# A hybrid decoder step: DeltaNet's keys, queries and values and the other heads' decayed keys turned by VectorE and DMA instead of TensorE

## Chip, core and metric

The kernel runs on one core of one Trainium2 chip. The time is the device time of one execution in microseconds (us); lower is better. A core has TensorE (PE: matmuls; PEld: its weight loads), VectorE (DVE), ScalarE (ACT), GpSimd (POOL) and SyncE (SP), which here issues every DMA. Each engine works off a queue of its own in order.

## What is computed

One layer of a decoder whose 16 heads are of three kinds, on 16 meta tokens + 1024 prompt tokens and on 8 samples of 8 tokens. Everything is float32; D is 2048 and a head has 128 channels.

```python
h = rmsnorm(x) ; proj = h @ w_in                      # 2048 x 8984
# 6 mLSTM heads (A): q, k, v, o and two gates; chunked, state C (128x128), n, m
P = exp(Dm - mt) * (q @ k.T);  num = a * (q @ C) + P @ v;  C_new = a_s * C + (w * k).T @ v
# 6 gated DeltaNet heads (B): a convolution of width 4 and silu over q, k, v, then q, k L2-normed
M = I + strict_tril(beta * decay * (k @ k.T));  solve M [U, Wk] = [beta v, beta e^G k]
W = U - Wk @ S;  o = e^G q @ S + Aqk @ W;  S_new = e^Ge S + (k e^(Ge-G)).T @ W
# 4 HGRN2 heads (C): per-channel forget gates
S_new = e^be S + (k e^(be-b)).T @ v
y = headRMSNorm(concat(heads)) * out_norm_w * silu(z);  out = x + y @ w_out  -> final rmsnorm
```

## The kernel before

The tokens are cut into two halves: half 0 has 80 sample and meta tokens (a small group) and 512 prompt tokens, half 1 the other 512 prompt tokens. The 512 are worked as a main group of four chunks of 128 (`NC = 4`). Activations lie with channels on partitions and tokens along the row; the recurrences also need some of them the other way round, a chunk's 128 tokens on partitions.

**Projection.** For each half, head by head in `ORDER` and tile by tile (k, q, v, o, z and so on; 128 columns of `w_in` each), `run_group` multiplies 16 slices of 128 rows. The weights come in pieces of four slices, 128x512: `w_raw` (and `o_raw` for `w_out`) loads a piece into a buffer `wraw` of the pool `wp` (four buffers), `feed_split` splits it into `whi` (ACT) and `wlo` (DVE, subtracting), and three products per slice go to `acc` (`oacc` for the output projection). `feed_ahead`, in the middle of each piece, lets the split run three pieces ahead and the load seven.

**Scans.** When a head's tiles are done, a generator (`mlstm_scan`, `gdn_scan`, `hgrn_scan`) does its recurrence. Its steps are woven between the weight matmuls by a planner (`Weave`, `Clock`) that adds up costs per engine while the program is written: a step runs when its due time, `ck.last + 0.4`, is reached on the planned TensorE clock; some steps set `ck.last` later. Scans run one after another in a queue; `finish` (the head's norm and gate) and `conv_post` (DeltaNet's convolution and silu) have queues of their own. `start_head` lets the head before the previous one run out (`weave.drain`). The framework then fixes the order of every engine's queue when the program is built.

**Row-wise tiles.** Two ways are in use. On TensorE: four transposes against `ident` into a PSUM bank, as for `pk` (mLSTM's k), `pck`, `pcq`, `pvb` (DeltaNet's k, q, v) and `pkh` (HGRN's decayed k). By VectorE and DMA, as for the values of mLSTM and HGRN, mLSTM's o and the scans' outputs: `V.transpose` turns 32x32 blocks, `turn_out` stores them to DRAM in four DMAs that put the blocks in place, and `turn_in` loads the turned tile in one.

**Buffers.** A tile's tag names its slot. Main-group tiles `gt("0")` to `gt("9")` have one slot each (`s0` to `s9`), shared by all scans; `kwall` and `Ball` share `sB`.

Of the kernel before, what the change touches and what calls it, by code (L numbers as in the profile page):

```python
# [14 lines left out]
P = 128  # L15
# [16 lines left out]
SQ = 32  # L32
# [159 lines left out]
def hybrid_step(ctx, tc, i, o):  # L192
# [25 lines left out]
    def bank(name):  # L218
        return ps.tile([P, 512], F32, tag="ps", name=name)
# [9 lines left out]


    def w_raw(col, g):
        raw = wp.tile([P, 512], F32, tag="wraw", name="wraw")
        v = raw.rearrange("p (k c) -> p k c", c=P)
        if col is None:
            V.memset(raw, 0.0)
            for src, at in ((C_AI, 0), (C_BB, 32), (C_AF, 64), (C_BA, 96)):
                DMA(v[:, :, at:at + HA], i["w_in"][0, 512 * g:512 * (g + 1), src:src + HA].rearrange("(k p) c -> p k c", p=P))
        else:
            DMA(v, i["w_in"][0, 512 * g:512 * (g + 1), col:col + P].rearrange("(k p) c -> p k c", p=P))
        return raw  # L240

    def o_raw(k, cg):
        raw = wp.tile([P, 512], F32, tag="wraw", name="wraw")
        DMA(raw, i["w_out"][0, P * k:P * (k + 1), 512 * cg:512 * (cg + 1)])
        return raw

# [182 lines left out]
    DMA(prows[0:72, :], i["gdn_conv_w"][0].rearrange("j (e c) -> (j e) c", c=P))  # L429
    DMA(prows[72:88, :], i["out_norm_w"][0].rearrange("(e c) -> e c", c=P))  # L430
    DMA(prows[88:92, :], i["hgrn_lower_bounds"][0].rearrange("(e c) -> e c", c=P))
    gsc = cp.tile([P, 1], F32, name="gsc")
    gbi = cp.tile([P, 1], F32, name="gbi")
    gn = cp.tile([P, 1], F32, name="gn")
    gli = cp.tile([P, 1], F32, name="gli")
    for t in (gsc, gbi, gn, gli):
        G.memset(t, 0.0)
    G.memset(gsc[RF], -1.0)
# [359 lines left out]
                S.activation(t[:, off:off + cnt], a, func, scale=scale)  # L798
        return t

    def turn_out(t, name):

        d = dp.tile([NC * NQ, SQ, NQ, SQ], F32, name=name)
        for q in range(NQ):
            DMA(d[:, :, q].rearrange("x j i -> j x i"), t[SQ * q:SQ * (q + 1), 0:HALF].rearrange("p (x i) -> p x i", i=SQ))
        return d
# [4 lines left out]
    def turned_evac(half, acc, tag, name, small):  # L811
        t = row(tag, name)
        for a, off, cnt in spans(half, acc):
            n = min(cnt, HALF - off)
            V.transpose(t[:, off:off + n], a[:, 0:n])
            if n < cnt:
                small(t[:, HALF:off + cnt], a[:, n:cnt])
        return t, turn_out(t, scratch_name(name))

    scratch_names = []  # L820

# [9 lines left out]
    def finish(half, head, outs, ssq, scale, zs):  # L831
        r = sp.tile([P, 16], F32, tag="hr", name="hr")
        for g in half.groups:
            V.tensor_scalar(r[0:g.n, g.idx], ssq[0:g.n, g.idx], scale / P, EPS, op0=ALU.mult, op1=ALU.add)
            G.tensor_tensor(r[0:g.n, 8 + g.at:8 + g.at + g.nt], r[0:g.n, g.idx], halfneg[0:g.n, 0:g.nt], op=ALU.pow)
        yield
        hrs = []
        for g, hx in zip(half.groups, outs):
            hr = gt("6", g)
            rb = r[0:g.n, 8 + g.at:8 + g.at + g.nt].unsqueeze(2).to_broadcast([g.n, g.nt, P])  # L840
            V.tensor_tensor(hr[0:g.n], hx[0:g.n], rb, op=ALU.mult)
            hrs.append(hr)
# [3 lines left out]
        d = turn_out(y, scratch_name("yd"))  # L846
# [118 lines left out]
    def mlstm_scan(half, h, kT, qT, vT, tho, zs, nm, em, st):  # L965
# [10 lines left out]
        Cn = state_A[h]  # L976
        Es, kws, v1s, ogs, hxs = [], [], [], [], []
        kwall = sp.tile([P, 5, P], F32, tag="sB", name="kwall", bufs=1)
        for g in half.groups:
            n = g.n  # L980
            pst = bank("pst")
            for c in range(g.nt):
                T.matmul(g.psum(pst, n)[:, c], g.col(kT, c), g.col(qT, c), start=True, stop=True)
            E = gt("0", g)
            for c in range(g.nt):
                S.activation(E[0:n, c, 0:n], g.col(nm, c)[0:n], AF.Exp, bias=cols[0:n, g.at + c, K_A, h:h + 1])
            ck.sync()
            V.tensor_tensor(E[0:n, :, 0:n], E[0:n, :, 0:n], g.psum(pst, n), op=ALU.mult)
            Es.append(E)
        yield  # L990
        for g in half.groups:
            n = g.n
            pk = bank("pk")
            for c in range(g.nt):
                T.transpose(g.psum(pk)[:, c], g.col(kT, c), ident)
            kw = kwall[:, g.idx]
            V.tensor_tensor(kw[0:n], g.psum(pk), gate_col(half, g, K_W, h), op=ALU.mult)
            kws.append(kw)
            v1 = gt("2", g, P + 1)
# [107 lines left out]
        G.tensor_copy(U[:, 0:3], hist[:, ei])  # L1107
        return U

    def conv_post(half, U, ei, Cv):  # L1110
        base = NB * (NS + 3)
        W = half.width
        co = sq("io", "co")
# [27 lines left out]
        yield  # L1141
        yield
        silu2(Cv[:, 0:W], U[:, 0:W], Cv[:, 0:W])

    def gdn_scan(half, h, ck_, cq, cv, zs, Gb, eG, bb, st):
        W = half.width
# [4 lines left out]
        qd = row("k", "qd")[:, 0:W]  # L1151
        nrm = sp.tile([P, 40], F32, tag="nrm", name="nrm", bufs=1)
        V.memset(nrm, 1.0)
        pks = []
        for g in gs:
            pk, pq = bank("pck"), bank("pcq")
            for c in range(g.nt):
                T.transpose(g.psum(pk)[:, c], g.col(ck_, c), ident)
            for c in range(g.nt):
                T.transpose(g.psum(pq)[:, c], g.col(cq, c), ident)  # L1160
            for off, src in ((0, pk), (5, pq)):
                for c in range(g.nt):
                    scr = sq("scr", "scrq", bufs=1)
                    S.activation(scr[0:g.n], g.psum(src)[:, c], AF.Square, accum_out=nrm[0:g.n, off + g.at + c:off + g.at + c + 1])
# [6 lines left out]
        yield  # L1171
        kns, Es = [], []
        for g, pk in zip(gs, pks):
            kn = gt("4", g)
            V.tensor_tensor(kn[0:g.n], g.psum(pk), nrm[0:g.n, 20 + g.at:20 + g.at + g.nt].unsqueeze(2).to_broadcast([g.n, g.nt, P]), op=ALU.mult)
            kns.append(kn)
        for g in gs:
            E = gt("0", g)
# [73 lines left out]
        def side():  # L1252
# [156 lines left out]
    def hgrn_scan(half, h, kT, lf, qT, vT, zs, st):  # L1409
# [97 lines left out]
        for g in gs:  # L1507
# [18 lines left out]
        Ss = gt("4", main)  # L1526
# [66 lines left out]
    def done_tile(half, name, what, acc):  # L1593
# [23 lines left out]
        elif kind == "B":  # L1617
# [5 lines left out]
            c["posts"].append(weave.add("post", conv_post(half, U, ei, t[what]), lag="V"))  # L1623
        else:
            if what == "f":
                cf = evac(half, acc, "f", "cf")[:, 0:half.width]
# [200 lines left out]
```

## Time and profile before

| | |
|---|---|
| median of 3 runs | 2525.41 us (2525.31 to 2526.97) |
| the profiled execution | 2525.14 us, its span 2523.4 us |
| PE busy | 2456.8 us (97%), 15702 matmuls |
| PEld / DVE / ACT / POOL busy | 2199.6 / 1427.0 / 1012.3 / 555.0 us |
| DMA engines | 53.9% for the queue that carries the data, 139 GB/s |
| half 0's projection and scans | to about 1185 us; half 1's to about 2118; then the output projection |

A line of a group reads: code line, engine, operation, tiles written <- read, shapes, count | busy time, mean ns of one | idle time of the engine before them and what ended it. All engine operations have one code line (L138), the helper that records them, so tiles tell them apart. Timeline rows give start, length, engine and operation, and in brackets how long the engine had been idle and what released it. "L239 <- DVE wlo" among SP's waits reads: the issue at line 239 waited for VectorE's instruction on wlo.

### The profile page before, as it was taken

What the parts mean: (1) busy time and instruction counts of PE and PEld (TensorE: products, weight loads), DVE (VectorE), ACT (ScalarE), POOL (GpSimd) and SP (SyncE); (2) the same over time, 40 slices, a digit from 0 to 9 for tenths busy, and PEclk for the clock granted to TensorE, in tenths of its full rate; (3) what the DMA queues carried; (4) which work ended last, traced back from release to release, by engine and by line L of the source; (5) the groups of instructions that cost most, each with busy time, mean ns of one, the idle gap of its engine ahead of it and who ended that gap; (6) DMA issues with size and microseconds to landing.
All of it is one profiled execution on the core that took longest, in us unless ns stands there. A gap on an engine that the chain in (4) does not pass through costs nothing.

```text
span 2523.4 us, 43205 instructions
## 1 busy us (share of the span) xinstructions
PE 2456.8 (97%) x15702; PEld 2199.6 (87%) x15702; DVE 1427.0 (57%) x2977; ACT 1012.3 (40%) x2476; POOL 555.0 (22%) x722
## 2 busy tenths in 40 slices
PE   6999999999999999999899999999999999999998
PEld 5899999999999999999687888888888888888886
DVE  7775656765746655556854556554554645323435
ACT  5643434343435333343643434333543334322324
POOL 5331211420314212213320103110320102211201
PEclk9999999999999999999999999999999999999999
DMA  5666655656545454448455445454554548636735
GB/s 129 157 143 147 154 135 122 166 135 133 144 97 143 97 128 115 118 105 225 115 134 122 119 121 130 120 132 100 131 128 111 130 118 264 175 83 195 259 96 184
DMA packets 681041, 350.77 MB, mean 139 GB/s; under 512 B 260004, under 2 KB 622076, under 8 KB 680828
## 3 DMA queue, kind: packets, MB, share of 16 engines
q1 hardware_dynamic: 680828, 348.01, 53.9%
q8 instruction: 123, 2.02, 0.3%
q14 instruction: 90, 0.74, 0.1%
HBM read 285.71 MB, written 62.19 MB: 138 GB/s over the span
## 4 chain that ended last, share of the span: by engine, by line
PE 74%; DMA 6%; issue 6%; DVE 5%; ACT 4%; POOL 3%; SPq 1%; POOLq 0%; DVEq 0%; ACTq 0%
PE acc L138 55%; PE oacc L138 8%; PE pa L138 1%; DVE wlo L138 1%; DMA wraw<-in_w_in_dram 1%; PE po L138 1%; POOL X L138 1%; PE pyy L138 1%; PE pz L138 1%; POOL res L138 1%; ACT whi L138 1%; PE pu L138 1%; ACT L138 1%; PE poh L138 1%; PE nd L138 1%
## 5 line engine op out<-in xcount | busy, mean ns | idle before, releaser
L138 DVE TENSOR_TENSOR wlo<-wraw,whi 128x512 fp32r<-128x512 f32 x720 | 528.4, 738 | 584.9 <-ACT whi L138 566.0
L138 PE MATMUL acc<-hA,whi 128*128 128x288 f32 (+1 forms) x4544 | 823.0, 303 | 11.5 <-ACT whi L138 7.0
L138 ACT CAST whi<-wraw 128x512 fp32r<-128x512 f32 x720 | 441.3, 618 | 879.8 <-PE acc L138 570.2
L138 PE MATMUL acc<-hB,whi 128*128 128x512 f32 x2272 | 723.8, 400 | 4.4 <-ACT whi L138 3.2
L138 PEld LDWEIGHTS acc<-hA,whi 128*128 128x128 f32 x4544 | 678.3, 191 | 17.5 <-ACT whi L138 8.4
L138 PE MATMUL acc<-hA,wlo 128*128 128x288 f32 x2240 | 488.9, 298 | 2.1 <-DVE wlo L138 2.0
L138 PEld LDWEIGHTS acc<-hB,whi 128*128 128x128 f32 x2272 | 411.2, 189 | 84.0 <-ACT whi L138 4.0
L138 PE MATMUL acc<-hB,wlo 128*128 128x512 f32 x1120 | 440.5, 393 | 5.1 <-DVE wlo L138 4.9
L138 PEld LDWEIGHTS acc<-hA,wlo 128*128 128x128 f32 x2240 | 367.1, 190 | 2.9 <-DVE wlo L138 2.9
L138 PE MATMUL oacc<-whi,y 128*128 128x512 f32 x1088 | 344.8, 391 | 1.7 <-ACT whi L138 1.6
L138 PEld LDWEIGHTS acc<-hB,wlo 128*128 128x128 f32 x1120 | 210.6, 188 | 55.9 <-DVE wlo L138 10.4
L138 PEld LDWEIGHTS oacc<-whi,y 128*128 128x128 f32 x1088 | 205.0, 188 | 45.6 <-ACT whi L138 3.4
L138 PE MATMUL oacc<-wlo,y 128*128 128x512 f32 x576 | 225.5, 392 | 2.1 <-DVE wlo L138 2.1
L138 PEld LDWEIGHTS oacc<-wlo,y 128*128 128x128 f32 x576 | 108.6, 189 | 26.1 <-DVE wlo L138 3.9
L138 POOL TENSOR_TENSOR res<-res,fnw 128x512 f32<-128x512 f32 (+1 forms) x34 | 54.3, 1624 | 255.3 <-ACT oscr L138 255.3
L138 POOL TENSOR_TENSOR qd<-qT,emb 128x512 f32<-128x512 f32 x12 | 16.8, 1403 | 355.9 <-PE po L138 355.9
L138 POOL TENSOR_TENSOR y<-y,zs 128x592 fp32r<-128x592 f32 (+1 forms) x32 | 45.5, 1420 | 92.4 <-ACT zs L138 62.8
L138 DVE TENSOR_TENSOR Yt<-Yc,Bb 128x60 f32<-128x60 f32 (+8 forms) x180 | 36.7, 204 | 39.4 <-DMA Bb<-db 34.4
L138 POOL TENSOR_TENSOR hr<-hr,halfneg 128x4 f32<-128x4 f32 (+1 forms) x48 | 47.4, 987 | 46.2 <-DVE hr L138 44.7
L138 POOL TENSOR_TENSOR X<-Ex,hk 128x256 f32<-128x256 f32 (+1 forms) x40 | 38.1, 953 | 87.8 <-PE pa L138 67.9
L138 POOL TENSOR_TENSOR nrm<-nrm,halfneg 128x10 f32<-128x10 f32 x12 | 23.5, 1955 | 122.6 <-DVE nrm L138 122.6
L138 DVE TENSOR_TENSOR Sx<-Sx,lf 128x256 f32<-128x256 f32 (+2 forms) x60 | 36.5, 613 | 20.2 <-ACT Ex L138 19.1
(410 smaller groups left out, 2805.8 us busy)
## 6 DMA issues: line engine op xcount, KB each, us to landing
wraw<-in_w_in_dram SPq DMA_DIRECT2D x564, 256.0 KB
wraw<-in_w_out_dram SPq DMA_DIRECT2D x144, 256.0 KB
y<-y SPq DMA_DIRECT2D x16, 576.0 KB
px<-in_x_prompt_dram SPq DMA_DIRECT2D x32, 256.0 KB
yd<-y SPq DMA_DIRECT2D x128, 64.0 KB
out_dram<-sst SPq DMA_DIRECT2D x16, 512.0 KB
s<-yd SPq DMA_DIRECT2D x32, 256.0 KB
y<-zs SPq DMA_DIRECT2D x32, 256.0 KB
```

Source lines behind the costliest of these rows:

```text
L138: return f(out, *a, **k)
```

## The change

Five tiles that were transposed on TensorE for the main group take the other way: DeltaNet's k, q, v, mLSTM's k, HGRN's decayed k. The small group of half 0 keeps TensorE. `turn` is new: a VectorE transpose into `uT` (one buffer) and `turn_out`. For DeltaNet it stands at the end of `conv_post`; the loads stand at the start of `gdn_scan`, with a yield and a due time 7 us later before the norms. In `mlstm_scan` the key's transpose stands ahead of the first matmuls, and the loads of k, v and o move into a step of their own after them, with a due time of 6 us. In `hgrn_scan` transpose and load are in one step, followed by 6 us. `wraw` gets a fifth buffer, and four single-column tiles become one tile of four columns.

```diff
     def w_raw(col, g):
-        raw = wp.tile([P, 512], F32, tag="wraw", name="wraw")
+        raw = wp.tile([P, 512], F32, tag="wraw", name="wraw", bufs=5)
...
-    gsc = cp.tile([P, 1], F32, name="gsc")
-    gbi = cp.tile([P, 1], F32, name="gbi")
-    gn = cp.tile([P, 1], F32, name="gn")
-    gli = cp.tile([P, 1], F32, name="gli")
+    gpar = cp.tile([P, 4], F32, name="gpar")
+    gsc, gbi, gn, gli = (gpar[:, n:n + 1] for n in range(4))
...
+    def turn(src, d):
+        t = sp.tile([P, HALF], F32, tag="uT", name="uT", bufs=1)
+        V.transpose(t, src)
+        turn_out(t, d)
+        return d
...
 # mlstm_scan
+        dk = turn(kT[:, 0:HALF], turn_tile("kd"))
         for g in half.groups:
...
             Es.append(E)
+        ck.last += 2.0
+        yield
+        v1m, og = gt("2", half.main, P + 1), gt("3", half.main)
+        turn_in(kwall[:, half.main.idx], dk)
+        turn_in(v1m[:, :, 0:P], vT[1])
+        turn_in(og, tho[1])
+        ck.last = ck.t["T"] + 6.0
         yield
         for g in half.groups:
             n = g.n
-            pk = bank("pk")
-            for c in range(g.nt):
-                T.transpose(g.psum(pk)[:, c], g.col(kT, c), ident)
-            kw = kwall[:, g.idx]
-            V.tensor_tensor(kw[0:n], g.psum(pk), gate_col(half, g, K_W, h), op=ALU.mult)
+            kw = pk = kwall[:, g.idx]
+            if g.small:
+                pk = bank("pk")[:, 0:P].unsqueeze(1)
+                T.transpose(pk[0:n, 0], g.col(kT, 0), ident)
+            V.tensor_tensor(kw[0:n], pk[0:n], gate_col(half, g, K_W, h), op=ALU.mult)
...
-            else:
-                turn_in(v1[:, :, 0:P], vT[1])
-                og = gt("3", g)
-                turn_in(og, tho[1])
 # conv_post, its last step
         silu2(Cv[:, 0:W], U[:, 0:W], Cv[:, 0:W])
+        turn(Cv[:, half.base:half.base + HALF], turned)
 # gdn_scan
+        (ck_, dk), (cq, dq), (cv, dv) = ck_, cq, cv
...
-            pk, pq = bank("pck"), bank("pcq")
-            for c in range(g.nt):
-                T.transpose(g.psum(pk)[:, c], g.col(ck_, c), ident)
-            for c in range(g.nt):
-                T.transpose(g.psum(pq)[:, c], g.col(cq, c), ident)
+            if g.small:
+                pk, pq = (bank(n)[0:g.n, 0:P].unsqueeze(1) for n in ("pck", "pcq"))
+                T.transpose(pk[:, 0], g.col(ck_, 0), ident)
+                T.transpose(pq[:, 0], g.col(cq, 0), ident)
+            else:
+                pk, pq, vm = gt("4", g), gt("9", g), gt("3", g)
+                turn_in(pk, dk)
+                turn_in(pq, dq)
+                turn_in(vm, dv)
+                ck.last = ck.t["T"] + 7.0
+                yield
...
-            kn = gt("4", g)
-            V.tensor_tensor(kn[0:g.n], g.psum(pk), nrm[...], op=ALU.mult)
+            kn = gt("4", g) if g.small else pk
+            V.tensor_tensor(kn[0:g.n], pk, nrm[...], op=ALU.mult)
...
-                pv = bank("pvb")
-                for c in range(g.nt):
-                    T.transpose(g.psum(pv)[:, c], g.col(cv, c), ident)
-                vb = gt("3", g)
-                V.tensor_tensor(vb[0:n], g.psum(pv), gate_col(half, g, K_HB, h), op=ALU.mult)
+                if g.small:
+                    pv = bank("pvb")[0:n, 0:P].unsqueeze(1)
+                    T.transpose(pv[:, 0], g.col(cv, 0), ident)
+                    vb = gt("3", g)
+                else:
+                    pv = vb = vm
+                V.tensor_tensor(vb[0:n], pv, gate_col(half, g, K_HB, h), op=ALU.mult)
 # hgrn_scan
+        dk = turn(kd[:, 0:HALF], turn_tile("kd"))
         for g in gs:
-            pt = bank("pkh")
-            for c in range(g.nt):
-                T.transpose(g.psum(pt)[:, c], g.col(kd, c), ident)
             kk = gt("3", g)
-            S.copy(kk[0:g.n], g.psum(pt))
+            if g.small:
+                pt = bank("pkh")
+                T.transpose(g.psum(pt)[:, 0], g.col(kd, 0), ident)
+                S.copy(kk[0:g.n], g.psum(pt))
+            else:
+                turn_in(kk, dk)
             kks.append(kk)
+        ck.last = ck.t["T"] + 6.0
         yield
```

More of the change, by code (lines that the diff above doesn't have):

```diff
@@ L242, in o_raw @@
     def o_raw(k, cg):
-        raw = wp.tile([P, 512], F32, tag="wraw", name="wraw")
+        raw = wp.tile([P, 512], F32, tag="wraw", name="wraw", bufs=5)
         DMA(raw, i["w_out"][0, P * k:P * (k + 1), 512 * cg:512 * (cg + 1)])
@@ L799, in evac, with turn_tile, turn_out @@
         return t
-    def turn_out(t, name):
-        d = dp.tile([NC * NQ, SQ, NQ, SQ], F32, name=name)
+    def turn_tile(name):
+        return dp.tile([NC * NQ, SQ, NQ, SQ], F32, name=scratch_name(name))
+    def turn(src, d):
[3 more added lines that the diff above has]
+        return d
+    def turn_out(t, d):
         for q in range(NQ):
@@ L817, in turned_evac @@
                 small(t[:, HALF:off + cnt], a[:, n:cnt])
-        return t, turn_out(t, scratch_name(name))
+        return t, turn_out(t, turn_tile(name))
     scratch_names = []
@@ L845, in finish @@
         V.transpose(y[:, 0:HALF], hrs[-1].rearrange("p c e -> p (c e)"))
-        d = turn_out(y, scratch_name("yd"))
+        d = turn_out(y, turn_tile("yd"))
         ck.last += 2.0
@@ L992, in mlstm_scan @@
             n = g.n
-            pk = bank("pk")
-            for c in range(g.nt):
-                T.transpose(g.psum(pk)[:, c], g.col(kT, c), ident)
-            kw = kwall[:, g.idx]
-            V.tensor_tensor(kw[0:n], g.psum(pk), gate_col(half, g, K_W, h), op=ALU.mult)
+            kw = pk = kwall[:, g.idx]
[3 more added lines that the diff above has]
+            V.tensor_tensor(kw[0:n], pk[0:n], gate_col(half, g, K_W, h), op=ALU.mult)
             kws.append(kw)
-            v1 = gt("2", g, P + 1)
+            v1 = gt("2", g, P + 1) if g.small else v1m
             G.memset(v1[0:n, :, P:P + 1], 1.0)
@@ L1108, in conv_evac, with conv_post @@
         return U
-    def conv_post(half, U, ei, Cv):
+    def conv_post(half, U, ei, Cv, turned):
         base = NB * (NS + 3)
@@ L1163, in gdn_scan @@
                     scr = sq("scr", "scrq", bufs=1)
-                    S.activation(scr[0:g.n], g.psum(src)[:, c], AF.Square, accum_out=nrm[0:g.n, off + g.at + c:off + g.at + c + 1])
+                    S.activation(scr[0:g.n], src[:, c], AF.Square, accum_out=nrm[0:g.n, off + g.at + c:off + g.at + c + 1])
             pks.append(pk)
@@ L1173, in gdn_scan @@
         for g, pk in zip(gs, pks):
[L1174 to L1175 removed]
+            kn = gt("4", g) if g.small else pk
+            V.tensor_tensor(kn[0:g.n], pk, nrm[0:g.n, 20 + g.at:20 + g.at + g.nt].unsqueeze(2).to_broadcast([g.n, g.nt, P]), op=ALU.mult)
             kns.append(kn)
@@ L1622, in done_tile @@
             t[what] = row({"k": "c", "q": "d", "v": "f"}[what], "C" + what)
-            c["posts"].append(weave.add("post", conv_post(half, U, ei, t[what]), lag="V"))
+            d = turn_tile("cd")
+            c["posts"].append(weave.add("post", conv_post(half, U, ei, t[what], d), lag="V"))
+            t[what] = t[what], d
         else:
```

## The prediction, made before the changed kernel had run

> **What bounds the kernel now.** I read the page first (busy shares), then the busy time by stretch, the waits of PE, the groups of the instructions that the change touches, and the timeline around them.
>
> ```profile
> PE 2456.8 (97%) x15702; PEld 2199.6 (87%) x15702; DVE 1427.0 (57%) x2977; ACT 1012.3 (40%) x2476; POOL 555.0 (22%) x722
> ```
>
> ```profile
> 650.00:700.00 50.00, 50.00 (x378) 49.81 (x377) 33.14 (x64) 20.36 (x61) 15.71 (x22) 1.00 0.57 148
> ...
> 1150.00:1200.00 50.00, 48.50 (x337) 43.73 (x335) 28.43 (x53) 14.85 (x34) 17.75 (x18) 1.00 0.88 247
> ...
> 2350.00:2400.00 50.00, 50.00 (x222) 41.40 (x221) 19.61 (x31) 14.45 (x28) 5.95 (x4) 1.00 0.83 279
> ```
>
> ```profile
> PE acc L138 <- ACT whi L138: 10.2, 8, 3.0
> PE acc L138 <- DVE wlo L138: 6.9, 8, 1.4
> ```
>
> The columns of the stretches are PE, PEld, DVE, ACT and POOL busy, PE's clock, the share of the DMA engines and GB/s. In stretches as far apart as 650 and 2350 us PE is busy for all 50 us, and its longest waits on the split weights come to 10.2 and 6.9 us in the whole run. So TensorE is the bound from end to end. An instruction taken off PE is worth its own time there, as long as nothing new makes PE wait. That is the whole question here.
>
> **What PE loses.** The change takes the full-chunk transposes off PE. Heads are counted by the code: DeltaNet's k, q and v, 6 heads x 2 halves x 4 chunks = 48 each; mLSTM's keys, 48; HGRN's decayed keys, 4 x 2 x 4 = 32. The groups show those counts:
>
> ```profile
> L138 PE MATMUL pcq<-ident,Cq 128*128 128x128 f32 x48 | 7.2, 273 | 0.0
> L138 PE MATMUL pk<-ident,kT 128*128 128x128 f32 x48 | 7.2, 272 | 0.0
> L138 PE MATMUL pvb<-ident,Cv 128*128 128x128 f32 x48 | 7.2, 272 | 0.0
> L138 PE MATMUL pck<-ident,Ck 128*128 128x128 f32 x48 | 7.2, 272 | 0.0
> ...
> L138 PE MATMUL pkh<-ident,hkd 128*128 128x128 f32 x32 | 4.8, 272 | 0.0
> ```
>
> That is 224 transposes; the small first group keeps its own. What does one cost? Three readings: 272 ns from start to end; 7.2/48 = 150 ns of busy time, with overlaps counted once; and what it really pushes back. The timeline gives the last:
>
> ```profile
> 336.31 0.47 PEld L138 LDWEIGHTS pck<-ident,Ck 128*128 128x128 f32 x4
> ...
> 336.75 0.47 PEld L138 LDWEIGHTS pcq<-ident,Cq 128*128 128x128 f32 x4
> ...
> 337.19 0.57 PEld L138 LDWEIGHTS acc<-hA,whi 128*128 128x128 f32 x4
> ...
> 1575.95 0.60 PE L138 MATMUL pkh<-ident,hkd 128*128 128x128 f32 x4
> 1576.30 0.70 PE L138 MATMUL acc<-hB,whi 128*128 128x512 f32 x2
> ```
>
> In half 0 eight transposes hold the weight port from 336.31 to 337.19: 0.88/8 = 110 ns each. In half 1 four set the next matmul back by 1576.30 - 1575.95 = 0.35 us, 88 ns each; that start says nothing of how far the matmul itself is stretched, so I take half 0's 110 ns for all: 224 x 0.110 = **24.6 us** off the path. The ends are 88 ns, 19.7 us, and 150 ns, 33.6 us, which only the overlap speaks against. "TensorE: Matmul & The Clock Gate" of the Trainium skill, Part 4, gives a transpose about 275 ns in a kernel's context. The trace agrees for one instruction from start to end (272 ns); by that figure the sum would be 224 x 0.275 = 61.6 us, which the starts above, with consecutive ones overlapping, speak against.
>
> **What DVE, ACT and POOL get.** 56 transposes of 128x512 on DVE (36 DeltaNet, 12 mLSTM, 8 HGRN):
>
> ```profile
> L138 DVE STREAM_TRANSPOSE y<-s 128x512 f32<-128x512 f32 x32 | 22.6, 706 | 0.4
> ...
> L138 ACT COPY s<-pkh x8: 571/587/589, 165.2 to 2168.0; 128x512 f32<-128x512 f32 x8
> ```
>
> 56 x 0.706 = 39.5 us on an engine that is busy 1427 of 2523 us: nothing on the path. It can hold one split of weights back by 0.7 us; three split pieces lie ahead of PE, and without that cover it would cost 39.5 us. ACT loses eight copies of 0.587 us. The multiplies that read PSUM now read SBUF; same shapes, taken as zero. POOL gets nothing but earlier inputs.
>
> **What SP and the DMA engines get.** Each turn is four stores and one load, 280 DMAs, 56 x 0.5 MB = 29 MB.
>
> ```profile
> DMA packets 681041, 350.77 MB, mean 139 GB/s; under 512 B 260004, under 2 KB 622076, under 8 KB 680828
> ...
> q1 hardware_dynamic: 680828, 348.01, 53.9%
> ...
> SPq L239 <- DVE wlo L138: 606.2, 282, 6.7
> SPq L244 <- DVE wlo L138: 240.3, 119, 11.6
> ```
>
> One turn out is 128 x 16 = 2048 runs of 32 floats, one turn in 512 rows of 128 floats, so 143,360 packets more. By bytes the share goes from 53.9% to 58%, by packets to 65%. PE stayed full at a share of 0.83 (2350 to 2400 us), so I take zero; at 0.88 it lost 1.5 us of 50, with other causes in that stretch. "DMA: Bandwidth & Descriptors" of the Trainium skill, Specifications, says that transfers under 512 B fall below line rate because the DMA engine reads, changes and writes back; the 2048 runs of each turn out are of that kind, and 260,004 of today's packets are too, with PE full all the same. SP, which issues everything, stands 606 + 240 us waiting for VectorE to release a raw weight buffer: that is its slack. The added issues take 56 x (1.95 + 0.38) = 130 us (rows below). What is queued behind a store that waits for its VectorE transpose is the next weight load. The fifth buffer moves that load's release one piece earlier, which pays for such a block; by itself I give it zero (bounds: 0, and the 17 us of PE's two waits above; SBUF space is all it costs).
>
> **How long one turn takes,** from the same move that the kernel makes for its outputs:
>
> ```profile
> 637.34 1.95 SPq L805 DMA_DIRECT2D yd<-y  x4
> ...
> 640.77 0.38 SPq L809 DMA_DIRECT2D s<-yd  x1
> ...
> 1498.37 0.70 DVE L138 STREAM_TRANSPOSE y<-s 128x512 f32<-128x512 f32 x1
> ...
> 1505.64 0.37 SPq L809 DMA_DIRECT2D s<-yd  x1
> ...
> 1508.95 0.75 DVE L138 SCALAR_TENSOR_TENSOR y<-s,onw,zs 128x512 f32<-128x512 f32 x1 [0.26 <-DMA s<-yd]
> ```
>
> Transpose 0.70, four issues 1.95, landing of the last store at most 1.5 (640.77 - 637.34 - 1.95), load issued and landed 1508.95 - 1505.64 = 3.3: about 7.5 us, against 0.4 us on PE. So each consumer must be 7.5 us or more behind its source. Are they?
>
> ```profile
> L138 ACT ACTIVATE kT<-acc x18: 403/416/607, 201.0 to 2014.2; 128x288 f32<-128x288 f32 x6, 128x304 f32<-128x304 f32 x6, 128x512 f32<-128x512 f32 x6
> ...
> L138 PE MATMUL pk<-ident,kT x54: 270/272/273, 283.0 to 2077.7; 128*128 128x128 f32 x48, 128*80 128x128 f32 x6
> ...
> L809 SPq DMA_DIRECT2D s<-vT x12: 360/367/459, 276.4 to 2070.3; - x12
> ...
> 327.88 0.77 DVE L138 SCALAR_TENSOR_TENSOR Cv<-U,Cv 128x592 f32<-128x592 f32 x1 [0.25 <-ACT U L138]
> ...
> 356.05 0.74 PE L138 MATMUL pvb<-ident,Cv 128*80 128x128 f32 x5
> ...
> 161.49 1.47 POOL L138 TENSOR_TENSOR hkd<-Sx,hk 128x592 f32<-128x592 f32 x1
> ...
> 163.97 0.71 PE L138 MATMUL pkh<-ident,hkd 128*80 128x128 f32 x5
> ...
> 1192.29 1.50 POOL L138 TENSOR_TENSOR hkd<-Sx,hk 128x592 f32<-128x592 f32 x1 [2.14 <-PE pa L138]
> ...
> 1198.97 0.71 PE L138 MATMUL pkh<-ident,hkd 128*80 128x128 f32 x5
> ...
> 1557.57 1.31 POOL L138 TENSOR_TENSOR hkd<-Sx,hk 128x512 f32<-128x512 f32 x1 [2.23 <-ACT U L138]
> ```
>
> mLSTM: kT is there at 201 and first transposed at 283, last at 2014 and 2078: over 60 us. In the code the load of v stands behind those transposes, yet SP issued it at 276.4, so a queue takes what is ready ahead of what isn't; the key's turn will run early in the same way. DeltaNet: v is ready at 328.7 and first transposed at 356, 27 us on (k and q, whose tiles come first, are ready earlier still). The new yield of 7 us ahead of the norms lengthens the scan, not PE's work. HGRN: kd is ready at 1558.9 and transposed at 1575.95, 17 us; but in half 0's first head it is 163.0 to 163.97, 1 us, and in its last 1193.8 to 1198.97, 5 us. Taking half 1's first head for a third, I give these three 1 us each, 3 us (bounds 0, and 3 x 6.5 = 20 us if PE had nothing else to do; it has the next weights' matmuls, so nearer to the lower end).
>
> **Sum,** against the profiled execution's own 2525.1 us (0.3 us under the median of 2525.4): 2525.1 - 24.6 + 3.0 = **2503.5 us**.
>
> **Rivals.**
> *Slower: the keys' turn becomes mLSTM's wait.* At a tile's end the scan is sometimes sent through without weight matmuls between:
>
> ```profile
> 636.15 1.24 PE L138 MATMUL pst<-qT,kT 128*80 128x80 f32 x10
> 637.22 0.27 PE L138 MATMUL pk<-ident,kT 128*80 128x128 f32 x1
> ...
> 639.15 0.47 PE L138 MATMUL pum<-meta,kwall 80*128 80x137 f32 x2 [1.01 <-ACT v L138]
> ```
>
> If the turn starts only with the scan, `pum` waits 7.5 + 0.7 (the gate multiply) - 3.0 (636.15 to 639.15) = about 5 us there; over 12 scans 60 us, 2525.1 - 24.6 + 60 = 2560. It decides above 24.6/12 = 2 us a scan. For it: the code puts the transpose at the scan's start, with new due times behind it. Against: the load at 276.4. Half of that price, 2530, would still be slower. "VectorE: DVE Perf Modes" of the Trainium skill, Rules for kernel authors, sends a 128x128 transpose to TensorE when PSUM will do as its destination; that advice fits this rival.
> *No change: the handover eats it.* If each turn costs PE 24.6/56 = 0.44 us through late splits, blocked weight loads or full DMA engines, the time is 2525. For it: the stretch at 0.88. Against: 0.83 with PE full, and SP's slack.
> *More: the transposes cost their busy time,* 2525.1 - 33.6 = 2491.5, or even their whole length of 272 ns, 2525.1 - 224 x 0.272 = 2464. For it: the busy column. Against: the next instruction starts before the last one's end. (Part 4's figure would land at this far end.)
>
> **Chances.** As forecast, 2496 to 2512: 0.60. A part lost, 2512 to 2520: 0.14. No change: 0.10. Slower: 0.10. More, under 2496: 0.06, nearly all of it at the near end. About 0.2% (5 us) is what a measurement of this kernel tells from nothing: faster 0.80, same 0.10, slower 0.10. The range 2493 to 2520 leaves out the rivals on the long side.
>
> **What would show it.** PE: 224 matmuls and weight loads fewer, pck, pcq, pvb, pk and pkh only with 80 tokens, PE busy down by 25 to 34 us with the idle time unchanged near 67 us. DVE: 56 transposes into uT. DMA: 824,000 packets, 374,700 under 512 B. SP: the waits at the raw buffers shorter. Wrong, if PE shows waits of over 2 us at pum or puh, or acc waits for whi behind an ACT or DVE that waits for a turned load.

## The result: slower by 99 us

The changed kernel takes 2624.9 us (median of 4 runs, 2618.5 to 2629.8) against 2525.4 us before: ratio 1.039, 95% interval [1.0375, 1.0405]. The profiled execution is one of 2622.4 us with a span of 2620.6. The page after, its engines and its DMA queue:

```profile
PE 2466.7 (94%) x15478; PEld 2195.1 (84%) x15478; DVE 1477.9 (56%) x3033; ACT 1016.8 (39%) x2474; POOL 551.3 (21%) x722
...
q1 hardware_dynamic: 828668, 377.39, 57.3%
```

The work moved as announced: PE has 15702 - 15478 = 224 matmuls fewer, DVE 56 instructions more. But PE is *busier*, 2466.7 against 2456.8 us, and it stands idle for 2620.6 - 2466.7 = 153.9 us where it stood for 66.6. So the span's 97.2 us are 87.3 us of new waiting and 9.9 us of busy time. The removed transposes were 33.6 us of busy time (4 x 7.2 + 4.8 in the prediction's rows), so the busy time of what is left grew by about 43 us. The mean granted clock fell from 0.992 to 0.975, which on 2466.7 us would be about 42 us (an estimate). The stretches show why (columns as in the prediction: PE, PEld, DVE, ACT, POOL busy, PE's granted clock, DMA share, GB/s); the kernel before was full at a clock of 1.00 in 650 to 700 us:

```profile
650.00:700.00 50.00, 32.44 (x215) 31.68 (x215) 29.09 (x60) 13.82 (x37) 6.36 (x17) 0.85 0.63 136
700.00:750.00 50.00, 39.94 (x267) 37.96 (x268) 25.35 (x52) 15.15 (x42) 8.34 (x10) 0.85 0.67 146
750.00:800.00 50.00, 42.36 (x314) 41.54 (x313) 23.16 (x64) 15.83 (x44) 8.10 (x10) 0.90 0.61 148
```

Where PE stops, its clock falls too. Set against the kernel before at the same weight matmul, the changed kernel is 1.2 us late at its 3264th weight matmul (595 us), 58.7 us at the 4032nd (777 us), 84.6 us at the 6912th, just behind the hand-over to half 1, and 97 to 100 us at the end (the starts of the two records, subtracted). So over half of the loss falls into one stretch of under 200 us. What PE waited for after:

```profile
PE acc L138 <- ACT whi L138: 31.4, 13, 7.0
PE puh L138 <- DMA s<-kd: 18.6, 4, 7.2
...
PE acc L138 <- DVE wlo L138: 13.2, 15, 1.7
PE pkT L138 <- DVE t L138: 11.3, 5, 7.4
PE pum L138 <- DVE kwall L138: 10.3, 2, 8.3
PE pkT L138 <- DVE s L138: 10.1, 10, 1.5
```

Every kind of turned tile has its reader on this list: `puh` for HGRN's keys, `pkT` for DeltaNet's, `pum` for mLSTM's. The largest row, though, is the weights. SP's own waits, a row of the kernel before and two of the changed one:

```profile
SPq L643 <- ACT px L138: 9.7, 6, 2.7
```

```profile
SPq L239 <- DVE wlo L138: 368.0, 185, 6.9
...
SPq L641 <- ACT px L138: 70.8, 11, 16.8
```

SP's wait at the raw buffers fell from 606 to 368 us, as forecast. But another grew from 9.7 to 70.8 us, the longest from 2.7 to 16.8: that of the stores of half 1's prepared tokens (`prep_B` writes their split parts to `hbhi` and `hblo`, 128 stores in all, which are read at half 1's start). These stores, and the preparation that they belong to, are the key. In 560 to 760 us of the kernel before and of the changed one (count, durations in ns, first and last start):

```profile
L643 SPq DMA_DIRECT2D hbhi<-px x12: 430/498/1532, 567.3 to 631.2; - x12
...
L643 SPq DMA_DIRECT2D hblo<-xT x12: 487/505/1378, 580.2 to 642.3; - x12
```

```profile
L641 SPq DMA_DIRECT2D hbhi<-px x36: 303/485/944, 564.7 to 737.4; - x36
...
L641 SPq DMA_DIRECT2D hblo<-xT x36: 303/504/1851, 567.3 to 739.6; - x36
```

24 stores became 72: the preparation, put off behind the turns in SP's order, is caught up here in bursts of eight. And mLSTM's key turn of that time is caught between them. First VectorE's transpose and the four stores of its result, then the timeline up to the readers, both of the changed kernel (L811 is `turn_out`, L815 `turn_in`; in two later kernels they are L814 and L818):

```profile
L811 SPq DMA_DIRECT2D kd<-uT x4: 502/1142/2743, 683.9 to 688.3; - x4
L138 DVE STREAM_TRANSPOSE uT<-kT x1: 697/697/697, 563.1 to 563.1; 128x512 f32<-128x512 f32 x1
```

```profile
679.63 2.11 SPq L641 DMA_DIRECT2D hblo<-xT  x4
...
683.91 5.66 SPq L811 DMA_DIRECT2D kd<-uT  x4
689.62 0.56 SPq L239 DMA_DIRECT2D wraw<-in_w_in_dram  x1
...
690.42 0.62 ACT L138 CAST whi<-wraw 128x512 fp32r<-128x512 f32 x1 [1.70 <-DMA wraw<-in_w_in_dram]
...
691.09 0.61 PE L138 MATMUL acc<-hA,whi 128*128 128x288 f32 x1 [7.00 <-ACT whi L138]
...
693.13 0.44 SPq L815 DMA_DIRECT2D kwall<-kd  x1
...
703.63 0.69 DVE L138 TENSOR_TENSOR kwall<-kwall,cols 128x512 f32<-128x512 f32 x1
...
704.57 2.06 PE L138 MATMUL pum<-s,kwall 128*128 128x129 f32 x8 [8.28 <-DVE kwall L138]
```

The keys were transposed at 563.1 us, 120 us ahead, yet their stores went out at 683.9: SP takes its list in the order in which it was built, and 48 token stores and 21 weight loads, among others, stood in front. The stores then took 5.66 us instead of the usual 2, so the weight load behind them came late and PE lost 7.00 us at `acc`; the load of the turned keys came at 693.1, and PE lost 8.28 us at `pum`. Not all of these 8.28 us is the load's way: VectorE had no idle time just before its multiply at 703.63, as from 696.88 on it worked through the next head's convolution, which stands ahead in its list. The landing of the load is not in the trace, so the two can't be parted.

The stop before this one has another place. SP's and ScalarE's rows:

```profile
638.78 1.54 SPq L239 DMA_DIRECT2D wraw<-in_w_in_dram  x3
657.20 1.96 SPq L641 DMA_DIRECT2D hbhi<-px  x4
...
656.56 0.62 ACT L138 CAST px<-xT 128x512 fp32r<-128x512 f32 x1 [2.22 <-DVE xT L138]
657.09 2.17 ACT L138 CAST whi<-wraw 128x512 fp32r<-128x512 f32 x4
```

From 640.3 to 657.20 us SP issued nothing: next in its list was a token store whose source ScalarE cast only at 656.56, and the stores of mLSTM's keys, ready since 563.8, waited behind it. The weights that PE lacked were not behind it, though: ScalarE cast four pieces in a row from 657.09 on without waiting for a load. These casts stood behind the preparation's cast in ScalarE's list, and that one waited for VectorE's transpose. So the preparation that is caught up here holds up ScalarE and VectorE as well as SP, and PE stood still for 6.84 us.

A stop costs more than its own length. This is PE behind that one:

```profile
657.75 1.35 PE L138 MATMUL acc<-hA,whi 128*128 128x288 f32 x4 [6.84 <-ACT whi L138]
...
659.39 1.19 PE L138 MATMUL acc<-hA,whi 128*128 128x288 f32 x4
...
664.32 0.72 PE L138 MATMUL acc<-hA,whi 128*128 128x288 f32 x4
```

After 6.84 us of waiting, four matmuls take 1.35 and 1.19 us, and a few us later 0.72 as everywhere else. "TensorE: Matmul & The Clock Gate" of the Trainium skill, Why this matters for your kernels, warns of idle gaps above some 3 us between bursts, behind which the clock goes back to half; these rows agree. A long gap isn't needed, though: in the kernel before, behind a scan's short matmuls with gaps of at most 0.93 us, four such matmuls took 1.31 us at 204.03 us and 1.16 us at 205.61.

### The profile page after: what moved, and what is told of

Its sections match the earlier page's. It is cut to its first block, busy times and chain, and to the rows that moved or that the text cites. A ratio compares the mean times of both kernels' runs of the same rounds, so it can differ in the third digit from the quotient of the medians.

```text
span 2620.6 us, 43203 instructions
## 1 busy us (share of the span) xinstructions
PE 2466.7 (94%) x15478; PEld 2195.1 (84%) x15478; DVE 1477.9 (56%) x3033; ACT 1016.8 (39%) x2474; POOL 551.3 (21%) x722
## 3 DMA queue, kind: packets, MB, share of 16 engines
q1 hardware_dynamic: 828668, 377.39, 57.3%
## 5 line engine op out<-in xcount | busy, mean ns | idle before, releaser
L138 PEld LDWEIGHTS acc<-hA,whi 128*128 128x128 f32 x4544 | 685.3, 192 | 38.0 <-ACT whi L138 29.2
L138 ACT ACTIVATE scrq<-s 128x128 f32<-128x128 f32 x224 | 69.2, 309 | 18.4 <-DVE s L138 12.8
L138 POOL TENSOR_TENSOR vx<-v,quadmask 128x512 fp32r<-128x512 f32 x16 | 21.9, 1370 | 137.1 <-ACT v L138 90.7
```

Of the source, the lines that this page charges most:

```text
L138: return f(out, *a, **k)
```

## The experiments

Four theories, as the expectations name them. 1: a turn's own way (one uT buffer, SP, landing) is what PE waits for. 2: the planner's new waits of 6 and 7 us make the scans too long for the room between two heads. 3: the fifth buffer. 4, formed after the first eight runs: SP's one queue is too full, and its other users, above all the token stores, are displaced and jam. One caution holds for all: each edit makes the build order every engine's list anew, so differences do not add up exactly.

**The parts alone.** Each takes the fifth buffer and one part of the diff; the other parts are as before.

```
e1: bufs=5 for wraw, nothing else
e2: + conv_post's turn, gdn_scan's three turn_in and its 7 us
e3: + mlstm_scan's turn of kT, its loads in a step of their own and 6 us
e4: + hgrn_scan's turn of kd and its 6 us
```

> The kernel before with a fifth raw weight buffer and nothing else of the change. Theory 1 (the turns themselves cost: each goes through one uT buffer and SP's one queue in order, and what waits for it makes PE stop): the buffer is worth nothing, 2520 to 2528 us. Theory 2 (the plan: the new waits of 6 and 7 us make DeltaNet's scan longer than the room between two heads, so the drain at a head's start leaves PE without weights' work): the same, 2520 to 2528 us. Theory 3 (the fifth buffer lets SP bring weights earlier and puts them ahead of the small transfers in its queue): a good part of the 99 us is already here, above 2550 us.

Measured: 2526.0 us, ratio 1.0003 [0.9994, 1.0012]. The buffer does nothing; theory 3 falls.

> The fifth buffer and DeltaNet's 36 turns (keys, queries, values); mLSTM's and HGRN's keys are transposed by TensorE as before. It removes 144 of the 224 transposes, worth 15.8 us at 110 ns. Theory 2 (DeltaNet's scan is 7 us longer and is drained): most of the loss stays, 2570 to 2620 us. Theory 1 (each turn costs alike): 36 of 56 turns, so about 0.64 of the loss of 124 us that stands against the expected gain of 24.6, that is 2525 - 15.8 + 80 = about 2590 us; the two then differ by the gaps: by theory 2 PE stops at the heads' drains in half 0 (near 600 to 800 us and 870 to 1010 us) and mLSTM's pum has no part in it. If the turns only hurt together: 2505 to 2515 us.

Measured: 2586.6 us, 1.0238 [1.0221, 1.0255]: 60 us lost with 36 turns, inside theory 2's range and 3 us from theory 1's number, so of no use to part them. `pum` has a part in it (18.8 us in two rows of PE's waits), which theory 2 had ruled out.

> The fifth buffer and mLSTM's 12 turns of its keys, with the loads of values and output gates in the step after; DeltaNet and HGRN as before. It removes 48 transposes, 5.3 us at 110 ns. Theory 2 (DeltaNet's longer scan): no loss here, 2518 to 2526 us. Theory 1 (each turn costs alike, 2.2 us): 2525 - 5 + 27 = about 2547 us. The slower rival of the prediction (the scan waits about 5 us for the keys at pum): 2560 us.

Measured: 2519.9 us, 0.997 [0.9958, 0.9983]. mLSTM's turns gain, about what 48 transposes are worth (5.3 us); theory 1's price per turn is wrong here.

> The fifth buffer and HGRN's 8 turns of its decayed keys; mLSTM and DeltaNet as before. It removes 32 transposes, 3.5 us at 110 ns, and I gave 3 us back. Theory 2: 2522 to 2528 us. Theory 1 (2.2 us a turn): 2525 - 3.5 + 18 = about 2539 us.

Measured: 2556.6 us, 1.0122 [1.0107, 1.0137]. Only 8 turns, and 31 us: neither theory expected it. The first head shows the place:

```profile
169.22 0.71 DVE L138 STREAM_TRANSPOSE uT<-hkd 128x512 f32<-128x512 f32 x1 [2.12 <-POOL hkd L138]
...
169.96 1.39 SPq L811 DMA_DIRECT2D kd<-uT  x3
...
171.93 0.34 SPq L811 DMA_DIRECT2D kd<-uT  x1
172.37 4.65 SPq L239 DMA_DIRECT2D wraw<-in_w_in_dram  x3
177.19 0.38 SPq L815 DMA_DIRECT2D s<-kd  x1
...
180.56 2.04 PE L138 MATMUL puh<-s,s 128*128 128x128 f32 x8 [3.05 <-DMA s<-kd]
...
215.89 0.37 PE L138 MATMUL pkT<-ident,t 80*128 80x80 f32 x1 [5.47 <-DVE t L138]
```

From transpose to reader it is 11.3 us, of which the load stands 4.65 us behind three weight loads. PE waited, and a longer stop followed at DeltaNet's `pkT`, which waited for the norms with only six weight matmuls between the transposes and itself. Two stretches, with PE's clock in the third column from the end:

```profile
175.00:200.00 25.00, 21.95 (x159) 21.34 (x158) 15.05 (x34) 7.72 (x22) 5.41 (x7) 0.86 0.43 95
200.00:225.00 25.00, 18.65 (x118) 17.99 (x117) 8.47 (x19) 8.52 (x32) 4.99 (x6) 0.80 0.57 144
```

15 of this run's 31 us arise in about these 50 us.

**Waits without turns, turns without readers.**

```
e5: e1, and at the change's three places
+   ck.last = ck.t["T"] + 6.0   (7.0 in gdn_scan)
+   yield
    (all transposes stay on TensorE)
e6: four raw buffers; every turn and its load are made,
    loads go to tiles that nobody reads; no wait in the plan,
    all transposes stay on TensorE
```

> The kernel before with the fifth buffer and the planner's three new waits (6 us in mLSTM's scan, 7 us in DeltaNet's, 6 us in HGRN's) at the places where the change has them, and none of the turns: all 224 transposes stay on TensorE. Theory 2 (the plan: longer scans meet the drain at the next head's start): most of the loss without any turn, 2570 to 2620 us. Theory 1 (the turns' own way through DVE, SP and the landing is what PE waits for): within 5 us of before, 2520 to 2530 us.

Measured: 2572.2 us, 1.0202 [1.0183, 1.0221], at the lower end of theory 2's range. The planner's waits alone cost 48 us. How they do is open: PE's new waits are short (`pum` 11.4 us in nine, for nothing that the profile shows, and `pkT` 11.8 us in five; the kernel before has none of the first and 0.7 us at `pkT`), and stretches of over 5 us without a weight matmul, which a drain would make, are fewer than before (four against seven between 150 and 2150 us).

> All 56 turns are made as in the change (VectorE's transpose, four stores, one load each), but nothing reads what they bring and no step waits for it: the 224 transposes stay on TensorE, four raw buffers, no new waits in the plan. mLSTM's, HGRN's and DeltaNet's turned keys go to a tile nobody reads, DeltaNet's queries and values to the tiles of the change, which are written anew. Theory 1a (the load on DVE, SP and the DMA engines delays the weights, whoever reads): a good part of the loss, 2550 to 2620 us. Theory 1b (only what waits for a turn costs) and theory 2 (the plan): 2522 to 2535 us.

Measured: 2576.1 us, 1.0206 [1.0189, 1.0223]. Turns that nobody needs cost 52 us, most of it in the same stretch (lag 0.5 us at 594 us, 41 us at 760):

```profile
658.42 1.63 SPq L814 DMA_DIRECT2D kd<-uT  x3
...
665.04 0.51 SPq L818 DMA_DIRECT2D s<-vT  x1
...
668.55 2.06 PE L138 MATMUL pum<-s,kwall 128*128 128x129 f32 x8 [21.81 <-DMA s<-vT]
```

No reader waits for `kd` here; but mLSTM's load of v, which was there before the change, stands behind the turn's stores on SP, and they behind the token stores. That is theory 1a, by way of the queue.

> The changed kernel with its turns and steps, but without the 6, 7 and 6 us that the planner is told to let pass behind the loads. Theory 2: the scans are as short in the plan as before, so the drains cost no more than before; what is left is the real landing time of a turned load behind the step, 3 to 4 us for each of 32 scans at most: 2510 to 2600 us, below the changed kernel. Theory 1: the allowances hid part of the landing, so without them it is slower than the changed kernel, 2640 us or more.

The edit takes the three `ck.last = ...` lines out of the changed kernel and keeps the steps. Measured: 2620.9 us, 1.0383 [1.0367, 1.0398]: the same as the changed kernel, which neither theory had. What the plan gives back is lost elsewhere, a part of it at `pkT`, whose waits grew from 21.4 to 33.7 us; PE's waits of this run:

```profile
PE pkT L138 <- DVE t L138: 17.8, 4, 6.8
PE pkT L138 <- DVE s L138: 15.9, 6, 5.0
```

> The changed kernel with two buffers for VectorE's turned copy (uT) and four raw weight buffers, so that a turn doesn't wait until the four stores of the one ahead have landed (VectorE stood 4.0 us ahead of HGRN's transpose at 927 us for that). Theory 1 with the one buffer as its place: 20 to 60 us of the loss come back, 2560 to 2605 us. Theory 2, or SP's order as the place: within 10 us of the changed kernel, 2615 to 2635 us.

The edit is `bufs=2` for uT and four raw buffers. Measured: 2624.0 us, 1.0397 [1.0381, 1.0412]. The one buffer is not the place, though VectorE does wait for it.

**SP's queue.**

```
e9:  the new turns' stores and loads: nc.gpsimd.dma_start
e10: hbhi, hblo stores:               nc.gpsimd.dma_start
e11: prep_B is started at n == 36 instead of n == 19
e12: the new turns' stores and loads: nc.scalar.dma_start
```

> The changed kernel, but the stores and loads of the 56 new turns are issued by GpSimd instead of SP. Theory 4 (SP's one queue is full: behind the turns' issues the 128 stores that prepare half 1's tokens slip from 137 to 642 us before to bursts at 565 to 740 us, and turns, weights and stores then wait for one another): SP's order is as before again, half 0 loses nothing at 600 to 800 us, 2560 to 2585 us. Theory 1 (the way of a turn itself, wherever it is issued): 2605 to 2640 us.

Measured: 2828.8 us, 1.1198 [1.1179, 1.1217].

> The changed kernel, but the 128 stores of half 1's prepared tokens (hbhi, hblo) are issued by GpSimd instead of SP; the turns stay on SP. Theory 4: the 43 us between 590 and 770 us go, 2570 to 2590 us. Theory 1: within 10 us of the changed kernel, 2612 to 2635 us.

Measured: 2733.3 us, 1.0815 [1.0799, 1.0831]. Both miss every theory: issuing from GpSimd costs more than what it was to relieve. In the run with the turns on GpSimd (busy, mean ns, idle before):

```profile
L811 POOL DMA_DIRECT2D cd<-uT x144 | 96.4, 669 | 342.1 <-issue 270.1 <-DVE uT L138 22.2 <-DVE nrm L138 14.5
```

669 ns of busy time for each, and 270.1/144 = 1.9 us more in which GpSimd waits for nothing that the profile shows, while its own tiles come late (PE waited 20.4 us for `un` and 3.7 us for `hkd`). These two say nothing on theory 4.

> The changed kernel, but the preparation of half 1's tokens is started at tile 36 instead of 19; all DMAs stay on SP. In SP's order its last 64 of 128 stores then lie among weight loads 153 to 243 instead of 135 to 167, so they are spread over three times as many. Theory 4 (the crowding of stores on SP): 25 to 40 us come back, 2580 to 2600 us, and there is no stop near 690 to 770 us. Theories 1 and 2: within 10 us of the changed kernel, 2612 to 2635 us.

Measured: 2579.9 us, 1.0211 [1.0194, 1.0228]: 45 us come back from one number, slightly more than theory 4 had. In SP's list the first 48 stores stay where they were (142 to about 492 us), as the build puts them ahead of their place in the code; the last 64, which fell between 588 and 740 us, now fall between 633 and 987 us. The stretch that had 32.44 and 39.94:

```profile
650.00:700.00 50.00, 50.00 (x375) 49.71 (x374) 35.69 (x75) 18.92 (x55) 13.73 (x22) 1.00 0.70 172
700.00:750.00 50.00, 48.77 (x424) 47.66 (x422) 28.14 (x76) 19.50 (x58) 8.34 (x11) 1.00 0.47 104
```

Theory 4 is shown for this part: the preparation that is caught up fast is the place. PE is full at a DMA share of 0.70, higher than the changed kernel's 0.63 there, so it was the order of the work, not the DMA engines. The preparation's casts and transposes on ScalarE and VectorE move along with its stores, so this run doesn't tell SP's list from theirs. The gain isn't all kept: at the weight matmul that the kernel before runs at 950 us, e11 is 1.4 us behind it and the changed kernel 73 us, but from there to the one at 1230 us e11 loses 37 us more and the changed kernel 11. Whether the later stores or the turns cause that was not tried.

> The changed kernel, but the stores and loads of the 56 new turns are issued by ScalarE. Theory 4: SP's order is nearly as before and half 0's 40 to 50 us come back, but ScalarE, which casts every weight, now stands behind a turn's landing at times, so some of it is lost again: 2570 to 2610 us. Theory 1: 2610 to 2640 us.

Measured: 2585.7 us, 1.0239 [1.0224, 1.0254], as theory 4 had it: off SP's list the turns leave the token stores nearly where they were (the 64th at 439 us and the last at 717; in the kernel before at 373 and 642). ScalarE stood behind landing turns (8.6, 6.2 and 4.1 us in three of its groups); how much of the rest that explains was not tried.

**What is left, and which turns are worth having.**

```
e13: e11 with hgrn_scan as before
e14: mLSTM's keys and DeltaNet's values alone, prep_B from n == 28;
     vm = gt("3", main); turn_in(vm, dv) at gdn_scan's start, no new wait
     in it; keys, queries and HGRN's keys stay on TensorE
e15: e13 without the allowances of 6 and 7 us
e16: e14, and DeltaNet's k and q are turned for nobody (four raw buffers)
e17: e14 with prep_B from n == 19
e18: the kernel before with prep_B from n == 28
```

> The changed kernel with half 1's tokens prepared from tile 36 on (as in the run before last) and HGRN's keys transposed by TensorE as before. With the stores spread, 51 us of lag were left, of them 16 at the hand-over to half 1, where HGRN's last turn in half 0 waits, and 19 us of waits of puh for the turned keys. If HGRN's turn is too late for its reader: 2535 to 2555 us. If what is left is DeltaNet's longer scan alone: 2570 to 2585 us.

("The run before last" and the lag of 51 us are e11's.) Measured: 2568.8 us, 1.0167 [1.0146, 1.0188]. That is between the two answers. HGRN's turns are worth 11 us of e11's 53. What is left is put down to DeltaNet's keys and queries only because mLSTM's keys gained alone; the start at tile 36 is in it too, as 22 us are lost between 950 and 1230 us here.

> Of the change only mLSTM's keys and DeltaNet's values are turned (24 turns, 96 transposes less, 10.6 us at 110 ns), with the fifth buffer and half 1's tokens prepared from tile 28 on; DeltaNet's keys and queries and HGRN's keys stay on TensorE, no wait is put into their scans. These are the turns that are read 20 us and more behind their source. If the distance to the reader decides: 2510 to 2517 us, faster than before. If any turn costs by SP's time: 2530 to 2545 us.

Measured: 2515.3 us, 0.9962 [0.995, 0.9975]: faster than before, by 9.6 us [6.3, 12.6]. PE has 96 matmuls fewer and stays full where the changed kernel stopped:

```profile
PE 2442.0 (97%) x15606; PEld 2188.4 (87%) x15606; DVE 1440.2 (57%) x3001; ACT 1011.6 (40%) x2474; POOL 557.4 (22%) x722
```

> As the run with HGRN undone and the tokens prepared from tile 36, but without the 6 and 7 us that the planner lets pass in mLSTM's and DeltaNet's scans. If the longer plan of DeltaNet's scan is what is left (waits alone cost 48 us): 10 to 30 us faster than with them, 2515 to 2535 us. If the landing of the turned keys and queries is what is left: the same or slower, 2545 to 2570 us.

Measured: 2561.4 us, 1.0147 [1.0133, 1.0161], 7 us better than with the allowances: less than the plan's 10 to 30, and inside the landing's range, which said the same or slower. As in e7, what the plan gives back is lost in part at the reader:

```profile
PE pkT L138 <- DVE s L138: 16.0, 6, 5.1
...
PE pkT L138 <- DVE t L138: 12.1, 4, 4.1
```

> The run with mLSTM's keys and DeltaNet's values, and DeltaNet's keys and queries turned as well, but for nobody: stored and loaded as in the change, while TensorE still transposes them for the reader (four raw buffers, to make room for the tile that nobody reads). If the reader that stands right behind the load is what costs: 2512 to 2522 us, within 7 us of the run without them. If the traffic on SP and the DMA engines costs even with the token stores spread: 2530 to 2565 us.

Measured: 2543.6 us, 1.0078 [1.0062, 1.0093]: 28 us over e14, in the lower half of the traffic answer's range. The place is again a caught-up preparation, now between 750 and 905 us:

```profile
773.41 1.03 SPq L814 DMA_DIRECT2D kd<-uT  x2
...
777.53 0.38 SPq L818 DMA_DIRECT2D kwall<-kd  x1
...
788.95 1.41 PE L138 MATMUL pum<-s,kwall 128*128 128x129 f32 x5 [12.57 <-DVE kwall L138]
```

Here too VectorE came from other work straight to the multiply that `pum` waited for, so its list has a part in the 12.57 us. The other 25 us up to e13, in spite of 96 transposes less, hold the readers behind the load, the planned 7 us and the tokens from tile 36; no run parts them.

> The run with mLSTM's keys and DeltaNet's values, but with half 1's tokens prepared from tile 19 as in both kernels, so nothing but turns and the fifth buffer stands against the kernel before. If the gain is the 96 transposes' (10.6 us): 2512 to 2518 us, as with the tokens later. If the later tokens were needed: 2520 to 2530 us.

Measured: 2537.2 us, 1.0055 [1.0043, 1.0068]. A miss: the same 24 turns with the tokens from tile 19 lose 13 us; between 625 and 780 us it falls 26 us behind, the rest of the run wins some back. One stretch of this run, and then the same of e14:

```profile
700.00:750.00 50.00, 41.52 (x297) 39.88 (x296) 24.55 (x65) 13.71 (x32) 7.36 (x9) 0.93 0.53 126
```

```profile
700.00:750.00 50.00, 50.00 (x435) 48.72 (x434) 28.97 (x78) 16.83 (x40) 4.20 (x7) 1.00 0.56 118
```

> The kernel before with half 1's tokens prepared from tile 28 instead of 19, and nothing else. If the later tokens only undo what the turns did to the order on SP: no change, 2520 to 2528 us, and the gain of the run with mLSTM's keys and DeltaNet's values is the turns'. If the later tokens are a gain by themselves: 2510 to 2518 us.

Measured: 2524.1 us, 0.9998 [0.9989, 1.0007]. The later tokens are no gain by themselves; e14's gain is its turns', once the later tokens make room for them.

Counted in SP's issues of L239, the token stores from the 64th to the 128th stand among so many weight loads (a weight load gives PE about 4 us of work in half 0: 89 to 156 is 373 to 642 us of the kernel before):

| kernel | weight loads | how many | time |
|---|---|---|---|
| before | 89 to 156 | 67 | 2525 |
| changed | 135 to 167 | 32 | 2625 |
| e6, dead turns | 137 to 167 | 30 | 2576 |
| e17 | 119 to 167 | 48 | 2537 |
| e16 | 142 to 202 | 60 | 2544 |
| e14 | 119 to 200 | 81 | 2515 |
| e11 | 153 to 243 | 90 | 2580 |

Why the build puts the preparation behind the turns was not tried. In the two pairs that differ by its start alone, the changed kernel and e11, e17 and e14, the jam between 600 and 780 us goes when the stores are spread. The count by itself is no rule: e16 with 60 is 28 us over e14, the kernel before with 67 has no jam.

## Why the prediction was wrong, point by point

- *PE bounds from end to end; an instruction off it is worth its own time "as long as nothing new makes PE wait".* Right, and the condition is what failed.
- *24.6 us for 224 transposes, 110 ns each.* 224 matmuls are gone. e14 gained 9.6 us [6.3, 12.6] with 96 of them, 100 ns each [66, 131]; e3 agrees. In e14's profiled execution PE is busy 14.8 us less, 154 ns each, and idle 2.8 us more, so the gain may be net of new waits: the term's size stands, but between 110 ns and the upper end of 150 the runs don't decide. The 275 ns that "TensorE: Matmul & The Clock Gate" in the Trainium skill, Part 4, gives for a bf16 transpose would be 26 us for 96, over twice what e14 gained.
- *DVE's 39.5 us hidden.* No run speaks against it: e14 and e3 have more work on DVE and gain.
- *The fifth buffer at zero.* Right, e1.
- *SP and the DMA engines at zero, since SP waits 606 + 240 us for raw buffers.* This is the first step that failed. The waiting was slack in the mean, not at a place: the list has an order, and the 240 us lie in the output projection, where of the new turns only the last head's is issued. The prediction named the weight load as what is queued behind a turn's store; the token stores, and the casts and transposes of the same preparation on ScalarE and VectorE, it never named. Dead turns cost 52 us (e6), and spreading the tokens brought 45 us back (e11). That the DMA engines are not the limit was right: 57.3% over the run, and no loss in e11's stretch at a share of 0.70.
- *Consumers are far enough behind; 3 us for HGRN.* The second failure. For mLSTM's keys and DeltaNet's values it holds (e3, e14). HGRN cost 31 us alone and 11 us at the end: a turn took 11.3 us to its reader in e4's first head, not 7.5. In e4's eight scans its load went out 7.3 to 19.8 us behind the transpose, where the prediction's parts give 4.2, as it queues behind weight loads. And I had bounded three heads at 20 us "if PE had nothing else to do". PE's list is fixed, so it does wait. For DeltaNet's keys and queries I judged the source, ready early, and not the load, which stands at the scan's start with the norms right behind it.
- *"The new yield of 7 us lengthens the scan, not PE's work."* Wrong: the three waits alone cost 48 us (e5). With e7 and e15 it is a trade: leave the waits out of the plan, and PE waits longer at pkT. By what way the planned waits cost PE time stays open.
- *"A queue takes what is ready ahead of what isn't."* This is the premise under both failures. I inferred it from one load that was issued earlier than the code has it. That was the build's ordering, done once; on the chip the keys ready at 563 us went out at 683.9.
- *The rivals.* The slower one had the right reader, `pum`, in the wrong cause: not a transpose that starts late but stores that stand in a queue, at 2 of its places (10.3 us, with VectorE's own list in the longer one); mLSTM by itself gained. The other readers, pkT and puh, had no rival. "VectorE: DVE Perf Modes" of the Trainium skill, Rules for kernel authors, which keeps a 128x128 transpose on TensorE when PSUM will do, fits e2 and e4, and not e3 and e14, whose readers on TensorE are far. A tenth for slower was too little for 280 DMAs on one ordered queue.
- *What a stop costs.* The prediction priced a wait at its length. In the changed kernel some 43 us of busy time come on top: the remaining matmuls ran longer, by about as much as the lower mean clock would give.

## What to carry to other kernels

An engine's waiting time, summed over the run, is not room at the place where new work goes: before adding DMAs to an ordered queue, list who else issues there, which of them has no near due time, and look where it will be caught up. Move a transpose off the bounding engine only where that engine's reader stands well behind the *load*, not only behind the source: in e14 `pum` comes 26 to 41 us behind the load of mLSTM's keys, in the changed kernel `puh` 3 to 9 us behind that of HGRN's. Here 24 turns of 56 were worth keeping, and with the background stores spread they gave 9.6 us. Price each stop of TensorE at its length and the slower matmuls behind it.

## What the runs showed of the hardware that I had not expected

A DMA issued by GpSimd held it for 0.67 us, and about 1.9 us more went by for each store in which it did nothing that the profile shows; SP issues the same store in about 0.5 us. Moving 280 of them there cost 204 us (e9 against the changed kernel), while ScalarE issued them at a gain of 39 us (e12).
